# Two feed-forward layers as seven half-size block products each, with activations and block sums kept in DRAM

## The chip, the cores and the metric

The program runs on one core of one Trainium2 chip. The metric is the device time of one execution in microseconds (us). The engines are named as in the profile: PE is TensorE (PEld its weight loads), DVE is VectorE, ACT is ScalarE, POOL is GpSimd and SP is SyncE, which issues most DMAs. SBUF is the on-chip memory with 128 partitions, PSUM the eight accumulators ("banks") of 128 x 512 float32 that PE writes.

## What is computed

Two transformer layers and one state-space block work on 1024 tokens of 1024 features, all in float32. Each of the two layers ends in a gated feed-forward part, and this is what the change touches:

```python
D_FF = 2816
def swiglu(h, w_in, w_out):
    gu = h @ w_in                       # [1024, 1024] @ [1024, 5632]
    gate, up = jnp.split(gu, 2, axis=-1)
    return (jax.nn.silu(gate) * up) @ w_out      # [1024, 2816] @ [2816, 1024]
# in each layer
    h = rmsnorm(x, norm_ffn[i]) * (1 + sc2) + sh2
    x = x + g2 * swiglu(h, ffn_w_in[i], ffn_w_out[i])
```

The first layer's attention (windowed) stands before its feed-forward part, the second layer's (dilated) between the two feed-forward parts, and the state-space block behind the second. That block needs tables made from its parameters alone (discretised matrices, rotations, Toeplitz strips).

## The kernel before

Activations are feature-major: a tile holds 128 features and 512 tokens (half of the tokens, called half 0 and half 1). A float32 product is made as three passes: each operand is split into a rounded part "hi" (a copy on ACT, L448) and the rest "lo" (a subtraction, mostly on DVE, L449), and PE adds hi hi, hi lo and lo hi into one bank. One pass is a matmul of 128 x 128 weights against 128 x 512 activations.

`ffn` (L1054) walks over the 22 tiles of 128 columns of D_FF in ten chunks. For a tile it loads the gate and the up columns, splits them, runs `col_gemm_steps` (L496, matmuls L502 to L504) for both halves of the tokens over eight tiles of features, applies the gate (L1082 to L1087), and at the end of a chunk `row_gemm` (L508, matmuls L488 to L490) multiplies the chunk's activations with its rows of w_out and adds to x in SBUF (L520). So there are 22 x 2 x 2 x 8 x 3 = 2112 matmuls into the hidden width and 22 x 8 x 2 x 3 = 1056 out of it, 3168 in a layer.

At each chunk's end one step of other work is called (`extra`): in the first layer the modulation vectors of the second (`adas`, 48 blocks of 512 KB loaded through tag `wr` and summed on DVE, L268), in the second the tables of the state-space block (`ssm_params`, L1104, written to DRAM: `scalars` on small tiles, `combo` L1303 and L1305, `rots` L1356 to L1362).

The norm ahead of a feed-forward part (`norm`, L385) is a generator that is advanced during `row_gemm` of the attention's output: squares of x, their column sums (PE, L368), 1/rms (small DVE steps, L332 to L339), its spreading over the partitions (PE, L379), then for each of eight feature tiles a scaling (DVE, L428), hi (ACT, L439) and lo (DVE, L442). The later half's last steps stay in `pending` and run during the first matmuls of `ffn`. The norm behind the second layer is `mix_norm` (L1390, L1391, L1406, L1409).

A planner orders each engine's instructions: of those that are ready by its own account, the one that stands first in the program goes first. At run time each engine and each DMA queue works in that fixed order. Tiles of one tag share a fixed number of buffers: 28 slabs of 128 x 1024, two each of `wr`, `wh`, `wl`, `o4` and `tmp`, four each of `s` and `pt`.

## Time and profile before

| | |
|---|---|
| time, median of three runs | 2835.63 us (2835.03 to 2835.66) |
| profiled execution, first to last instruction (span) | 2824.5 us |
| the median beyond that span | 11.1 us |
| PE busy | 2696.7 us, 95% of the span |
| DVE busy | 1648.9 us, 58% |
| ACT busy | 996.4 us, 35% |
| POOL busy | 406.3 us, 14% |
| DMA | 235.97 MB, mean 84 GB/s |

The first feed-forward part lies at about 448 to 1185 us, the second at 1645 to 2375 us. A busy share is an average over all stages; what a stage is worth has to be read from windows inside it.

### The profile page before, as it was taken

What the parts mean: (1) busy time and instruction counts of PE and PEld (TensorE: products, weight loads), DVE (VectorE), ACT (ScalarE), POOL (GpSimd) and SP (SyncE); (2) the same over time, 40 slices, a digit from 0 to 9 for tenths busy, and PEclk for the clock granted to TensorE, in tenths of its full rate; (3) what the DMA queues carried; (4) which work ended last, traced back from release to release, by engine and by line L of the source; (5) the groups of instructions that cost most, each with busy time, mean ns of one, the idle gap of its engine ahead of it and who ended that gap; (6) DMA issues with size and microseconds to landing.
All of it is one profiled execution on the core that took longest, in us unless ns stands there. A gap on an engine that the chain in (4) does not pass through costs nothing.

```text
span 2824.5 us, 32756 instructions
## 1 busy us (share of the span) xinstructions
PE 2696.7 (95%) x12494; PEld 2208.4 (78%) x12494; DVE 1648.9 (58%) x3031; ACT 996.4 (35%) x1820; POOL 406.3 (14%) x518
## 2 busy tenths in 40 slices
PE   4999999999999999988899899999999999999998
PEld 4777778888888888767787678888788887988877
DVE  7788776555564333565666777465554636266355
ACT  4577643111111112377888431111111123224231
POOL 1355521000000000123333200000100003020000
PEclk8999999999999999999999999999999999999999
DMA  7332331333341112211122321121221221261131
GB/s 269 102 97 87 124 101 46 104 117 114 117 129 45 45 45 75 75 38 39 39 61 55 121 61 45 60 69 66 78 69 60 69 75 49 86 209 52 42 144 61
DMA packets 234141, 235.97 MB, mean 84 GB/s; under 512 B 53912, under 2 KB 195968, under 8 KB 233600
## 3 DMA queue, kind: packets, MB, share of 16 engines
q1 hardware_dynamic: 228272, 214.91, 24.6%
q0 software_dynamic: 5312, 18.88, 2.1%
q8 instruction: 98, 1.61, 0.2%
q14 instruction: 59, 0.48, 0.1%
q10 hardware_dynamic: 400, 0.09, 0.0%
HBM read 197.51 MB, written 34.24 MB: 82 GB/s over the span
## 4 chain that ended last, share of the span: by engine, by line
PE 77%; DVE 10%; ACT 5%; DMA 3%; issue 3%; POOL 2%; SPq 0%; ACTq 0%; DVEq 0%; POOLq 0%
PE psg L503 13%; PE psg L502 13%; PE psg L504 13%; PE pssc L489 3%; PE pssc L488 3%; PE pssc L490 3%; PE pstp L488 3%; PE pstp L489 3%; PE pstp L490 3%; PE psg L488 3%; PE psg L490 3%; PE psg L489 3%; PE pso L682 2%; POOL s L136 2%; PE pstp L668 2%
## 5 line engine op out<-in xcount | busy, mean ns | idle before, releaser
L502 PE MATMUL psg<-hh,wh 128*128 128x512 f32 x1888 | 745.6, 396 | 2.8 <-ACT hh L439 2.3
L503 PE MATMUL psg<-hl,wh 128*128 128x512 f32 x1888 | 741.5, 393 | 3.3 <-DVE hl L442 3.2
L504 PE MATMUL psg<-hh,wl 128*128 128x512 f32 x1888 | 740.9, 393 | 1.1 <-DVE wl L449 1.1
L503 PEld LDWEIGHTS psg<-hl,wh 128*128 128x128 f32 x1888 | 357.3, 189 | 76.9 <-DVE hl L442 7.7
L504 PEld LDWEIGHTS psg<-hh,wl 128*128 128x128 f32 x1888 | 356.7, 189 | 76.2 <-DVE wl L449 1.9
L502 PEld LDWEIGHTS psg<-hh,wh 128*128 128x128 f32 x1888 | 356.8, 189 | 73.6 <-ACT hh L439 3.0
L448 ACT CAST wh<-wr 128x1024 fp32r<-128x1024 f32 (+1 forms) x150 | 152.4, 1017 | 608.3 <-PE psg L503 460.3
L449 DVE TENSOR_TENSOR wl<-wr,wh 128x1024 fp32r<-128x1024 f32 (+1 forms) x133 | 159.1, 1196 | 233.6 <-ACT wh L448 233.5
L1084 ACT ACTIVATE tg<-psg 128x512 f32<-128x512 f32 x88 | 52.3, 594 | 545.1 <-PE psg L504 543.6
L1082 DVE TENSOR_TENSOR tg<-tg,psg 128x512 f32<-128x512 f32 x88 | 60.4, 686 | 231.8 <-PE psg L504 231.7
L126 ACT ACTIVATE s<-s,nm 128x256 f32<-128x256 f32 (+4 forms) x320 | 162.5, 511 | 37.7 <-DVE nm L122 32.7
L399 POOL TENSOR_TENSOR nacc<-nacc,nsq 128x512 f32<-128x512 f32 x30 | 40.5, 1350 | 796.7 <-ACT nsq L397 796.6
L520 DVE SCALAR_TENSOR_TENSOR x<-pssc,hf,x 128x512 f32<-128x512 f32 x160 | 119.4, 746 | 58.3 <-PE pssc L490 57.9
L520 DVE SCALAR_TENSOR_TENSOR x<-pstp,hf,x 128x512 f32<-128x512 f32 x160 | 119.4, 746 | 53.1 <-PE pstp L490 52.9
L692 POOL TENSOR_TENSOR o<-o,ob 64x512 f32<-64x512 f32 x80 | 114.6, 1432 | 226.9 <-ACT o L691 220.2
L488 PE MATMUL pssc<-pt,o 128*128 128x512 f32 x352 | 139.4, 398 | 1.0 <-ACT pt L1086 0.7
L488 PE MATMUL pstp<-pt,o 128*128 128x512 f32 x352 | 138.2, 393 | 0.2 <-DVE x L520 0.2
L489 PE MATMUL pssc<-s,o 128*128 128x512 f32 x352 | 138.3, 393 | 0.0
L490 PE MATMUL pstp<-pt,o 128*128 128x512 f32 x352 | 137.6, 391 | 0.0
L490 PE MATMUL pssc<-pt,o 128*128 128x512 f32 x352 | 137.2, 390 | 0.0
L489 PE MATMUL pstp<-s,o 128*128 128x512 f32 x352 | 137.1, 390 | 0.0
L1085 DVE SCALAR_TENSOR_TENSOR tg<-tg,psg 128x512 f32<-128x512 f32 x88 | 60.1, 683 | 113.8 <-ACT tg L1084 113.8
(426 smaller groups left out, 4864.4 us busy)
## 6 DMA issues: line engine op xcount, KB each, us to landing
adaw<-in_ada_w_dram SPq DMA_DIRECT2D x96, 512.0 KB, 3.7
wr<-in_ffn_w_in_dram SPq DMA_DIRECT2D x88, 512.0 KB, 3.8
wr<-in_ffn_w_out_dram SPq DMA_DIRECT2D x44, 512.0 KB, 3.2
wr<-in_w_in_dram SPq DMA_DIRECT2D x24, 512.0 KB, 3.9
xs<-x SPq DMA_DIRECT2D x16, 512.0 KB, 4.0
x<-xs SPq DMA_DIRECT2D x16, 512.0 KB, 4.4
wr<-in_b_w_in_dram SPq DMA_DIRECT2D x12, 512.0 KB, 3.7
xraw<-in_x_dram SPq DMA_DIRECT2D x8, 512.0 KB, 4.7
```

The source lines that it names most:

```text
L126: self.net.nc.scalar.activation(s[:, 0:w], s[:, 0:w], AF.Exp, bias=self.nm[:, i:i + 1], scale=0.125, accum_out=self.l[:, i:i + 1])
L448: self.nc.scalar.copy(hi, raw)
L449: (eng or self.nc.vector).tensor_sub(lo, raw, fl(hi))
L488: nc.tensor.matmul(ps, whi, xhi, start=(a == 0), stop=False)
L489: nc.tensor.matmul(ps, whi, xlo, start=False, stop=False)
L490: nc.tensor.matmul(ps, wlo, xhi, start=False, stop=(a == n - 1))
L502: nc.tensor.matmul(ps, hi[:, k, :], xhi, start=(k == 0), stop=False)
L503: nc.tensor.matmul(ps, hi[:, k, :], xlo, start=False, stop=False)
L504: nc.tensor.matmul(ps, lo[:, k, :], xhi, start=False, stop=(k == KT - 1))
L520: nc.vector.scalar_tensor_tensor(xx, ps, g[:, m:m + 1], xx, op0=ALU.mult, op1=ALU.add)
L692: nc.gpsimd.tensor_add(oap, oap, b)
L1082: nc.vector.tensor_mul(th, th, ps)
```

## The change

Both products of a feed-forward part are made by Winograd's form of Strassen's scheme: the operands are cut into 2 x 2 blocks, and seven block products with sums of blocks replace the eight.

`ffn` becomes two functions. `ffn_wide` makes the hidden activations: tokens are cut in halves, features in halves, and gate against up columns take the place of the two column blocks. It needs seven forms of the normed input (B11, B21, T1 to T4, B22), which `block_norm` makes in place of `norm`: 28 slabs, so x leaves SBUF (to `xd`). For each of 22 column tiles seven products of 12 matmuls run; weight sums are made on POOL, hi and lo parts on ACT and DVE, and partial results are added outside PSUM. The gated activations go to DRAM (`acts`), and POOL also makes block sums of w_out, which go to DRAM as well (`sums`).

`ffn_narrow` multiplies by w_out in seven products of 11 steps with 12 matmuls each. Every step loads half a tile of weights or weight sums, forms block sums of activations on POOL, and splits both operands. x comes back from `xd`.

`adas` now runs in `ffn_wide` of the first layer, one block at every third product, through tag `wl`. `ssm_params` is cut in two parts: one in each `ffn_narrow`, listed by product, traced with a priority 1500 places back (`behind`); its tables pass through DRAM between the two. The norms behind take their tiles of half 1 in the order 4 to 7, 0 to 3, and run within the last product.

The diff, cut to its core (comments that it drops, and changes of names, are left out):

```diff
+    def block_norm(self, x, sb, done):
+        def plain(name, k, src):
+            hi, lo = parts(name, k)
+            nc.scalar.copy(hi, src)
+            nc.vector.tensor_sub(lo, src, fl(hi))
+        def half(hf, order=range(KT)):
...
+            for k in range(4):
+                for i in range(2):
+                    scaled(v[k][i], 4 * i + k, 1, R)
+                nc.vector.tensor_sub(v[k][0], v[k][0], u[k])
+                nc.vector.scalar_tensor_tensor(t2[k], v[k][1], sb(1)[:, 4 + k:5 + k], v[k][0], op0=ALU.add, op1=ALU.subtract)
+                plain("T2", k, t2[k])
+                yield
+            done(1)
+            for k in range(4):
+                plain("T1", k, v[k][0])
+                yield
+            for j in range(KT):
+                nc.vector.scalar_tensor_tensor(u[j], u[j], sb(1)[:, j:j + 1], t2[j % 4], op0=ALU.add, op1=ALU.subtract)
+                yield
+            for j in range(KT):
+                plain("T3" if j < 4 else "T4", j % 4, u[j])
+                yield
+            for k in range(4):
+                shifted("B22", k, 4 + k, v[k][1])
+                yield
-    def ffn(self, i, h, then, extra=()):
+    def ffn_wide(self, i, H, also):
...
+        def operand(at, q, n):
+            g, u = raws[q]
+            if n == 0:
+                sum1[q] = self.slab("tmp", name="sum1")[:, lo_half]
+                nc.gpsimd.tensor_add(sum1[q], u[:, lo_half], u[:, hi_half])
+                nc.gpsimd.tensor_sub(u[:, lo_half], u[:, lo_half], g[:, lo_half])
+            if n == 2:
+                nc.gpsimd.tensor_sub(g[:, lo_half], sum1[q], g[:, lo_half])
+            if n == 6:
+                nc.gpsimd.tensor_sub(g[:, hi_half], g[:, hi_half], g[:, lo_half])
...
+            nc.scalar.copy(t[:, lo_half], src)
+            nc.vector.tensor_sub(t[:, hi_half], src, fl(t[:, lo_half]))
...
+        def take(q, n):
...
+            if n in (0, 2, 4):
+                nc.scalar.copy({0: g0, 2: g1, 4: u0}[n], ps)
+            if n == 1:
+                nc.vector.tensor_add(g0, ps, g0)
+                gate(q, 0)
+            if n == 4:
+                nc.vector.tensor_add(u1, bank[q, "V"], u0)
+            if n == 5:
+                nc.vector.tensor_add(u0, ps, u0)
+                nc.vector.tensor_mul(u0, u0, g0)
+            if n == 6:
+                nc.vector.tensor_add(g1, ps, g1)
+                gate(q, 1)
+                nc.vector.tensor_mul(u1, u1, g1)
+                nc.sync.dma_start(acts[q], ev[q][:, 1, :])
+        def weight_sums(f):
...
+            nc.gpsimd.tensor_add(b[:, hi_half], b[:, hi_half], a[:, hi_half])
+            nc.gpsimd.tensor_sub(a[:, hi_half], a[:, hi_half], a[:, lo_half])
+            nc.gpsimd.tensor_sub(a[:, lo_half], b[:, hi_half], a[:, lo_half])
+            nc.gpsimd.tensor_sub(b[:, lo_half], b[:, lo_half], a[:, lo_half])
...
+        order = [(q, n) for q in range(2) for n in range(2)] + [(q, n) for q in range(2) for n in range(2, 7)]
+        order += [(q, n) for q in range(2, NF) for n in range(7)]
+        AHEAD = 7
...
+            if q > 1 and n == 3 and q % 2 == 0:
+                weight_sums(q // 2 - 1)
+            if q > 1 and at % 3 == 0 and also:
+                also.run(1)
...
+    def ffn_narrow(self, i, acts, sums, xd, then, also):
...
+        PRODUCTS = (
+            ("1", lambda f: w_out[f * P:(f + 1) * P, lo_half], s11, None, [(0, 0)]),
+            ("2", lambda f: w_out[(f + NK) * P:(f + NK + 1) * P, lo_half], s21, None, [(0, 0)]),
+            ("5", lambda f: sums[f, 1][:, hi_half], s11, s12, [(4, 1), (0, 1)]),
+            ("6", lambda f: sums[f, 0][:, lo_half], s11, s22, [(0, 1)]),
+            ("4", lambda f: w_out[(f + NK) * P:(f + NK + 1) * P, hi_half], s21, s11, [(4, 0)]),
+            ("7", lambda f: sums[f, 0][:, hi_half], s12, s22, [(4, 0), (4, 1)]),
+            ("3", lambda f: sums[f, 1][:, lo_half], s22, None, [(0, 1)]),
+        )
...
+            nc.gpsimd.tensor_sub(dst[f], a, b)          # combine(c), for 5, 6, 4, 7
...
+            for into, tag, t, eng in ((wpart, "pt", raw.pop(c), nc.gpsimd if name in "123" else nc.vector),
+                                      (bpart, "s", src[f], nc.vector)):
...
+                nc.scalar.copy(o[:, lo_half], t)
+                eng.tensor_sub(o[:, hi_half], t, fl(o[:, lo_half]))
+        FETCH, COMBINE, SPLIT = 7, 4, 3
...
+            if f % 2 and also.get(name):
+                with self.behind():
+                    also[name].pop(0)()
...
+                        nc.vector.scalar_tensor_tensor(xx, bk[m], gain[:, m0 + m:m0 + m + 1], xx, op0=ALU.mult, op1=ALU.add)
...
+        first = {"1": [load, scalars], "2": [do(couts, 0), do(rots, 0)], "5": [do(couts, 1)], "6": [do(bins, 0)], "4": [do(rots, 1)],
+                 "7": [do(toep, 0), save]}
+        second = {"1": [restore, do(bins, 1), do(toep, 1), do(bins, 2)], "2": [do(couts, 2), do(rots, 2)], "5": [do(couts, 3)],
+                  "6": [do(toep, 2)], "4": [do(rots, 3)], "7": [do(bins, 3), do(toep, 3)]}
```

## Rows read from the trace of the kernel before

**Rows 1.** The page, part 1: engine, busy us (share), instructions; span first.
```profile
span 2824.5 us, 32756 instructions
PE 2696.7 (95%) x12494; PEld 2208.4 (78%) x12494; DVE 1648.9 (58%) x3031; ACT 996.4 (35%) x1820; POOL 406.3 (14%) x518
```

**Rows 2.** Busy time by stretch: stretch and length, busy us (instructions), clock, DMA share, GB/s.
```profile
900.00:1000.00 100.00, 100.00 (x442) 82.50 (x441) 40.88 (x52) 13.50 (x16) 0.00 (x0) 1.00 0.12 37
1000.00:1100.00 100.00, 100.00 (x442) 82.48 (x441) 36.01 (x43) 16.00 (x19) 0.00 (x0) 1.00 0.16 48
```

**Rows 3.** Groups by line: out<-in, shapes, count, then busy us and mean ns.
```profile
L520 DVE SCALAR_TENSOR_TENSOR x<-pssc,hf,x 128x512 f32<-128x512 f32 x160 | 119.4, 746 | 58.3 <-PE pssc L490 57.9
L268 DVE SCALAR_TENSOR_TENSOR tmp<-adaw,cond,tmp 128x1024 f32<-128x1024 f32 x84 | 112.0, 1333 | 21.4 <-DMA adaw<-in_ada_w_dram 20.8
L1082 DVE TENSOR_TENSOR tg<-tg,psg 128x512 f32<-128x512 f32 x88 | 60.4, 686 | 231.8 <-PE psg L504 231.7
L1084 ACT ACTIVATE tg<-psg 128x512 f32<-128x512 f32 x88 | 52.3, 594 | 545.1 <-PE psg L504 543.6 <-DVE s L1087 1.5
L279 DVE TENSOR_REDUCE adar<-psg 128x4 f32<-128x512 f32 x12 | 8.1, 683 | 0.1
```

**Rows 4.** One line's instructions: duration in ns, shortest/median/longest (L399, engines POOL and DVE).
```profile
L399 POOL TENSOR_TENSOR nacc<-nacc,nsq x30: 1261/1294/1745, 409.5 to 1632.7; 128x512 f32<-128x512 f32 x30
L399 DVE TENSOR_TENSOR nacc<-nacc,nsq x12: 675/682/694, 422.1 to 1638.6; 128x512 f32<-128x512 f32 x12
```

**Rows 5.** Timelines of DVE and of POOL: start us, us, instruction; 2372 to 2375.
```profile
2372.76 0.75 DVE L1391 SCALAR_TENSOR_TENSOR nacc<-nsq,f,nacc 128x512 f32<-128x512 f32 x1
2373.46 1.75 DVE L1409 TENSOR_TENSOR xnl<-nu,xnh 128x512 fp32r<-128x512 f32 x1
2372.87 1.78 POOL L1390 TENSOR_TENSOR nacc<-nacc,nsq 128x512 f32<-128x512 f32 x1 [1.86 <-ACT nsq L1386]
```

**Rows 6.** Timelines of DVE and of POOL from 2031 us on.
```profile
2031.41 0.74 DVE L520 SCALAR_TENSOR_TENSOR x<-pssc,hf,x 128x512 f32<-128x512 f32 x1
2031.73 2.41 POOL L1305 TENSOR_TENSOR o<-o 128x1024 f32<-128x1024 f32 x1 [18.36 <-DVE o L1303]
```

**Rows 7.** DVE busy on tile `ws` in a stretch; groups by line of the state-space tables.
```profile
1680.00:1735.00 55.00, 23.59 (x141) 1.00 0.30 68
L1303 DVE TENSOR_TENSOR o<-xc,pw 128x1024 f32<-128x1024 f32 x16 | 19.0, 1221 | 1.6 <-DMA d_bin<-o 1.4
L1362 DVE TENSOR_TENSOR o<-o 128x8 f32<-128x8 f32 (+6 forms) x28 | 8.6, 307 | 0.1
L1305 POOL TENSOR_TENSOR o<-o 128x1024 f32<-128x1024 f32 x12 | 29.1, 2424 | 555.4 <-DVE o L1303 475.2 <-PE psg L504 49.2 <-ACT tg L1084 31.1
```

**Rows 8.** Timeline at the start of the first feed-forward part.
```profile
446.67 0.39 PE L502 MATMUL psg<-hh,wh 128*128 128x512 f32 x1
454.42 1.05 PE L379 MATMUL pso<-ident,rs_y 128*128 128x128 f32 x8
455.51 2.06 DVE L428 SCALAR_TENSOR_TENSOR nu<-x,sc,pso 128x512 f32<-128x512 f32 x3 [0.93 <-PE pso L379]
```

**Rows 9.** Busy time by stretch of 10 us behind each feed-forward part (columns of rows 2).
```profile
1190.00:1200.00 10.00, 7.84 (x32) 4.82 (x31) 7.82 (x12) 7.00 (x9) 0.00 (x0) 1.00 0.00 0
1200.00:1210.00 10.00, 8.11 (x30) 5.15 (x29) 9.39 (x12) 7.66 (x9) 0.00 (x0) 0.83 0.04 10
2380.00:2390.00 10.00, 4.28 (x27) 2.62 (x25) 10.00 (x13) 7.99 (x14) 2.33 (x3) 0.97 0.41 113
2390.00:2400.00 10.00, 8.89 (x41) 8.15 (x42) 6.25 (x15) 5.53 (x9) 3.23 (x5) 0.51 0.60 192
```

**Rows 10.** Busy time of the first 100 us (columns of rows 2); DMA issues, KB, us to landing.
```profile
0.00:100.00 100.00, 61.36 (x274) 51.28 (x275) 71.25 (x117) 43.31 (x70) 13.74 (x31) 0.85 0.62 219
xs<-x SPq DMA_DIRECT2D x16, 512.0 KB, 4.0
x<-xs SPq DMA_DIRECT2D x16, 512.0 KB, 4.4
```

343 lines of the change are left out of this document (251 added, 92 removed).

## The prediction

> **What bounds the kernel now.** I read the page's busy shares first: PE is busy for 95% of the span, DVE for 58%, POOL for 14% [rows 1]. Shares are averages, so busy time by stretch came next: inside a feed-forward part PE is busy in all of 100 us and ends 442 matmuls in it, one per 0.226 us, while DVE works about 40 of the 100 us and POOL not at all [rows 2]. So in these stages PE's count of matmuls sets the time, and a matmul taken away there is worth 0.226 us as long as nothing else becomes late. The other engines have room only on average and without POOL; what happens when POOL works beside DVE is read from two timelines [rows 5, 6].
>
> **What is taken away.** A layer's 3168 matmuls become 22 x 84 = 1848 in the wide half and 7 x 11 x 12 = 924 in the narrow half: 396 fewer, 792 in all. At 0.226 us that is 179 us, the whole gain. The moved steps (modulation vectors, state-space tables) keep their matmuls.
>
> **What a subtraction costs now.** The added work is DVE and POOL instructions of 128 x 512. Alone, DVE takes 0.68 us and POOL 1.29 us [rows 4]; DVE instructions in a row start 0.66 us apart (three in 2.06 us) [rows 8]. They don't run beside each other when DVE reads two tiles of SBUF: at 2372.76 L1391 starts on DVE, POOL's addition starts 0.11 us later and takes 1.78 instead of 1.29 us, and DVE's next, L1409, takes 1.75 instead of 0.68 us [rows 5]. The three last 2.45 us from first start to last end, against 0.75 + 1.29 + 0.68 = 2.72 us in sum: they ran one after the other, and the two hand-overs saved 0.27 us. The x update L520, which reads PSUM and one tile of SBUF, keeps its 0.74 us under a POOL addition [rows 6]. So I count DVE's two-tile instructions and POOL's as one resource ("the pair"): one of each takes 1.70 us, two of DVE and one of POOL 2.36 us.
>
> The Trainium skill, SBUF — State Buffer, section "Who interferes with whom", states the same as a rule: a DVE instruction with two SBUF inputs and a GpSimd instruction that reads SBUF exclude each other for the whole instruction, and it speaks against this change. The rows agree, but for the 0.27 us; by the rule to the letter, steps take 1.97 and 2.65 us, which is the slower rival below.
>
> **The wide half.** A column tile has 84 matmuls, 19.0 us. ACT has 12 instructions of 0.59 us [rows 3], 7.1 us: hidden. DVE has seven splits, two gates and two products that read two tiles of SBUF and four additions from PSUM; POOL has four block sums and, on average, two for w_out. The pair needs 6 x 1.70 + 5 x 0.66 = 13.5 us, the PSUM additions 4 x 0.66 = 2.6 us, half of it under POOL: 14.8 us. In the first layer `adas` adds 48 sums of 1.33 us and 12 reductions of 0.68 us [rows 3], 3.3 us a tile: 18.1 us. Both fit into 19.0, so the hidden products are PE-bound; operands are made seven products ahead. Not ahead is the third partial: behind product n=4 ACT copies (0.59), DVE adds (0.69), and only product n=5 (2.7 us) lies before n=6, which waits for it. If a locked pair (1.97) is queued before that addition, PE waits 3.25 - 2.71 = 0.5 us. I take that for every tile in the first layer and for a third of them in the second: 11 + 4 = 15 us. Bounds: 0, and 59 us if nothing overlaps (first layer 21.2 us a tile, 48 us; second 11 us by the chain alone).
>
> **The entries.** Now the feed-forward part starts while half 1 of the norm is under way: 1/rms is spread 8.8 us after the first matmul (446.67 to 455.5) [rows 8]. The new order has 48 matmuls (10.9 us) that need half 0 alone. Then T2 is wanted, and each of its four tiles costs DVE five instructions: 4 x 5 x 0.66 = 13.2 us, with about six splits and takes between them (4 us) ready at 26.0 us. T2's matmuls of two column tiles are 5.4 us, the last 1.4 behind that moment: PE ends them at 27.4 us after 16.3 us of work, 11.1 us idle. T1 follows at once; T3 needs four lows, eight sums and a split more (9 us, to 35.0), PE is through T1 at 32.8: 2.2 us idle. T4 and B22 then stay ahead. 13 us an entry. TensorE's clock can fall after such a stretch (0.51, that is its 1.2 GHz, in the 10 us behind one with PE 43% busy [rows 9]): 1 us more each. 28 us together; bounds 16 (the planner puts other splits behind the norm) and 50.
>
> **The narrow half** has 77 steps of 12 matmuls, 2.71 us, with operands only three steps ahead. In products 1, 2 and 3 DVE splits one operand and POOL the other: 1.70 us. In 5, 6, 4 and 7 DVE splits both and POOL makes a block sum: 2.36 us. Alone, both fit. But the six products before the last (179.1 us of PE) also carry:
> - 24 x updates, 15.8 us, half of them under POOL: 7.9 us;
> - half of the state-space tables. First layer: the small steps 23.6 us and six of 0.68 us, 4.1 us; four `combo` with 2.44 us on DVE and 2.42 us on POOL each; two `rots` of six lines at 8.6/4 us, 12.9 us each [rows 4, 7]: with 1 us of hand-overs off, 72 us. Second layer: eight `combo` and two `rots`, 63 us.
>
> Splits and sums take 22 x 1.70 + 44 x 2.36 = 141.2 us. Sums: 141.2 + 7.9 + 72 = 221 us, 42 over PE's time; 212 us, 33 over, in the second layer. The low priority doesn't help here: by DVE's own time alone (22 x 0.66 + 44 x 1.32 + 15.8 + 63 = 151 of 179 us) the tables fit, so a plan that leaves the exclusion out puts them there. DVE's queue is fixed, and PE waits behind it. 75 us; bounds 0, and 131 us without any overlap.
>
> **The last product and the norm behind.** Its 11 steps take 29.9 us of PE. The pair has 11 x 1.70 = 18.7 us, x updates 4 us, and the norm: in the first layer about 8 POOL additions, 8 L442, 8 L428 half hidden and 1/rms, 20 us; in the second `mix_norm` has a DVE sum to each square too, 30 us. Over by 13 and 23 us. The kernel before already loses 4 and 7 us there (PE idle in rows 9), so 9 and 16 more, of which I let the next stage's opening matmuls hide half: 12 us; bounds 0 and 51.
>
> **DMA.** Added per layer: w_out is read again in parts, block sums and activations are written and read, x too: about 60 MiB. The narrow half needs 23 MiB in the first 119 us, some 205 GB/s; the start of the program held 219 GB/s with the DMA engines 62% busy [rows 10]. All go through SP's queue, seven steps ahead: hidden. `adas` shares `wl` with the w_out sums; SP can stand behind a held buffer for about 13 us (load 4, four sums 5.2, store 4 us), and what is queued behind it, the next w_in load, is wanted a tile (19 us) later. At each seam the first tiles come back from DRAM as slabs fall free during the last tile's products: 2 us, 4 in all.
>
> **Sum.** 179 - (15 + 28 + 75 + 12 + 4 = 134) = 45 us off the profiled span: 2824.5 - 45 = 2779.5; with the 11.1 us by which the median lies above it, 2790.6, rounded to 2790 us, its own range 2740 to 2845.
>
> **Rivals.**
> - *PE stays the bound.* The tables and sums fall where DVE has room, since splits alone need 2.36 of 2.71 us and `behind` lets them slip. Against it: the planner's account above. Only entries and seams are lost: 2835.6 - 179 + 32 = 2689 us. Chance 0.22.
> - *Slower: VectorE and GpSimd one after the other.* Hand-overs save nothing, x updates find no cover, in the narrow half above all; 1.97 (0.68 + 1.29) and 2.65 us (2 x 0.68 + 1.29) a step. Losses: narrow 70 + 61, last product 51, wide 59, entries and seams 32, together 273: 2835.6 - 179 + 273 = 2930 us. It decides from where those two savings in the narrow half (132 x 0.28 = 37 and 16 us) are gone: then losses are 187 and exceed 179. For it: every hand-over in rows 5 is a block; against it: the 0.27 us and rows 6. Chance 0.18. (This is the Trainium skill's rule to the letter.)
> - *The round trip doesn't overlap, so the scheme doesn't do what it says.* Loads of `acts` wait for the last store: store 4.0, load 4.4 [rows 10], first split 1.3 us, 10 us a seam, 19 us: 2809 us. Against it: only one tile's store is late. Chance 0.08.
>
> **How the numbers follow.** The forecast has 0.52. The range reaches from the first rival to part of the slower one, 2685 to 2890 us, and leaves out about 0.2. A measurement of this kernel can tell about 0.2% (6 us) from no change. Faster by more than that: 0.44 of the forecast's 0.52, 0.22, and 0.06 of the last rival's, 0.72; within it 0.06; slower 0.22.
>
> **What would show it.** Right: some 84 matmuls per 19 us in the wide halves; in the narrow halves PE below 90% with DVE near 100% busy, splits of 128 x 512 lasting up to 2 us, and PE's waits put down to splits; about 13 us of PE idle behind each entry with DVE as releaser. Wrong: PE over 97% busy in the narrow halves (first rival); PE waiting for DMA at the seams (last); DVE full in the first layer's wide half too (slower). A DVE subtraction of two SBUF tiles that keeps 0.68 us beside POOL would make the sum wrong at its root.

## The result, and the profile after

The changed kernel takes 2955.2 us (2950.0 to 2959.9 in four runs), the kernel before 2835.3 beside it: 1.0425 times as long, 95% interval 1.041 to 1.0441. The forecast was 2790 us with a range to 2890: the sign was wrong, and the time lies 65 us outside. The gain itself came, 792 matmuls fewer; what the forecast had at 134 us of losses was far more.

The page of the changed kernel, parts 1 and 5 (as [rows 1] and [rows 3]):

```profile
span 2958.2 us, 33846 instructions
PE 2605.7 (88%) x11702; PEld 2109.5 (71%) x11702; DVE 2023.3 (68%) x3389; ACT 1259.5 (43%) x2416; POOL 1033.8 (35%) x936
...
L1173 DVE TENSOR_TENSOR wpart<-wraw,wpart 128x512 fp32r<-128x512 f32 x264 | 261.8, 994 | 83.7 <-ACT wpart L1172 82.1
```

TensorE falls from 95% to 88% busy, GpSimd rises from 14% to 35%. A split on VectorE, 0.68 us alone [rows 4], takes 0.99 us in the mean.

Busy time by stretch (columns as in [rows 2]): the first two column tiles of the first layer, a stretch late in the second wide half, product 2 of either narrow half, and product 3, the last, of either (a narrow half makes its products in the order 1, 2, 5, 6, 4, 7, 3):

```profile
453.60:490.00 36.40, 29.19 (x101) 21.73 (x102) 34.22 (x56) 15.38 (x28) 8.85 (x6) 0.81 0.12 38
490.00:516.00 26.00, 21.41 (x86) 16.63 (x85) 25.29 (x32) 10.76 (x19) 10.03 (x6) 0.93 0.32 103
2070.00:2170.00 100.00, 100.00 (x443) 82.84 (x442) 68.67 (x80) 36.81 (x63) 26.77 (x18) 1.00 0.24 77
990.00:1068.00 78.00, 36.94 (x143) 28.09 (x141) 51.42 (x181) 13.58 (x24) 43.46 (x34) 0.76 0.50 154
2225.00:2314.00 89.00, 43.68 (x167) 32.60 (x166) 34.89 (x31) 16.20 (x29) 47.09 (x31) 0.71 0.41 143
...
1208.00:1249.00 41.00, 36.12 (x164) 28.95 (x164) 31.53 (x49) 20.93 (x36) 15.97 (x12) 0.96 0.37 112
2456.00:2507.00 51.00, 40.65 (x181) 32.04 (x180) 34.16 (x53) 19.52 (x32) 19.28 (x14) 0.83 0.22 61
```

The third line is the forecast come true: 443 matmuls in 100 us, TensorE never idle. The fourth and fifth show where it failed. Product 2 has 132 matmuls, 29.9 us; it took 78.4 and 88.4 us, and VectorE was far from full in it (51 of 78, 35 of 89 us). TensorE stood idle for 41.1 and 45.3 us of it; the rest of the loss is the lower granted clock (0.76 and 0.71) and the tables' own matmuls.

To place the loss I count the matmuls of L1185 and L1356 by their start times: 84 are a column tile, 132 a product, and each piece is compared with 19.0 or 29.9 us.

| piece | first layer, us over | second layer, us over | forecast for both |
|---|---|---|---|
| column tiles 1 and 2 (36.4 + 26.0; 35.9 + 29.8) | 24 | 28 | 28 |
| column tiles 3 to 22 | 56 | 28 | 15 |
| products 1, 2, 5, 6, 4, 7 | 75 | 87 | 75 |
| product 3 and the norm | 11 | 21 | 12 |

Together 330 us. The kernel before lost 45 in the same parts: its 3168 matmuls of a layer took 733.3 and 744.2 us from first start to last, where 716 are needed (3168 at 0.226). So 285 us are new against a gain of 179; in the stages between, the two profiled executions differ by a further 25. In wide tiles 3 to 22 the loss comes in lumps, tiles of 25 to 28 us between tiles of 19 to 23. From tile 11 of the second layer on, behind the last weight sum, every tile takes 19.0.

What TensorE waits for in the first wide half, VectorE's longest wait there, and SP's own (us in total, times, longest):

```profile
PE pssc L1185 <- DVE ev L1205: 28.3, 10, 6.2
PE psg L1185 <- ACT ev L1200: 9.3, 4, 4.2
...
DVE tmp L267 <- DMA adaw<-in_ada_w_dram: 40.7, 19, 7.6
...
SPq L1155 <- DVE wpart L1173: 99.8, 36, 11.5
SPq L1224 <- POOL wsum L1222: 65.5, 11, 8.3
```

SP's issues around one lump in the second layer (start us, us):

```profile
1818.36 0.33 SPq L1219 DMA_DIRECT2D wsum<-in_ffn_w_out_dram  x1
1826.85 0.33 SPq L1224 DMA_DIRECT2D wsum<-wsum  x1
1827.22 0.43 SPq L1155 DMA_DIRECT2D wraw<-in_ffn_w_in_dram  x1
1828.21 0.52 SPq L1225 DMA_DIRECT2D wsum<-wsum  x1
1828.83 0.44 SPq L1155 DMA_DIRECT2D wraw<-in_ffn_w_in_dram  x1
```

SP stands from 1818.7 to 1826.9 at a store that GpSimd has yet to make. The w_in loads of the tile after next stand behind it. GpSimd, then ScalarE, then TensorE wait in turn; TensorE's wait at the end of this chain, at 1836, is 6.1 us, behind ScalarE's copy L1200. The store's queue is what readers should see here: no engine is full.

In the first layer the chain runs through `adas`. One lump there, on SP, VectorE and TensorE:

```profile
773.90 0.33 SPq L1224 DMA_DIRECT2D wsum<-wsum  x1
776.59 5.41 SPq L255 DMA_DIRECT2D adaw<-in_ada_w_dram  x3
...
780.35 1.29 DVE L267 SCALAR_TENSOR_TENSOR tmp<-adaw,cond,tmp 128x1024 f32<-128x1024 f32 x1 [7.62 <-DMA adaw<-in_ada_w_dram]
781.55 0.68 DVE L1205 TENSOR_TENSOR ev<-pssc,ev 128x512 f32<-128x512 f32 x1
...
782.29 3.89 PE L1185 MATMUL pssc<-H,wpart 128*128 128x512 f32 x10 [5.55 <-DVE ev L1205]
```

SP stands at a sum's store until 773.9 and issues the rows of `adas` behind it; VectorE waits 7.6 us for them, with the addition L1205 behind that sum, and TensorE waits for the addition.

Waits in product 2, of TensorE and VectorE, first layer and then second:

```profile
PE pso L1453 <- DVE o L1400: 20.5, 1, 20.5
...
DVE o L1397 <- DMA o<-in_ssm_log_dt_dram: 13.1, 1, 13.1
DVE o L1435 <- PE pso L1434: 11.0, 1, 11.0
...
PE pso L1599 <- POOL o L1591: 26.9, 2, 18.9
PE pso L1614 <- POOL o L1591: 8.7, 1, 8.7
...
DVE o L1589 <- DMA o<-ssmp: 24.5, 1, 24.5
```

All of these are steps of the state-space tables. TensorE stands in its own queue at a transpose whose data are not there, with the products' matmuls behind it.

### The profile page after: what moved, and what is told of

Read it like the earlier page. It is cut to its first block, busy times and chain, and to the rows that moved or that the text cites. A ratio compares the mean times of both kernels' runs of the same rounds, so it can differ in the third digit from the quotient of the medians.

```text
span 2958.2 us, 33846 instructions
## 1 busy us (share of the span) xinstructions
PE 2605.7 (88%) x11702; PEld 2109.5 (71%) x11702; DVE 2023.3 (68%) x3389; ACT 1259.5 (43%) x2416; POOL 1033.8 (35%) x936
## 5 line engine op out<-in xcount | busy, mean ns | idle before, releaser
L1185 PE MATMUL psg<-H,wpart 128*128 128x512 f32 x1584 | 405.4, 404 | 42.4 <-ACT ev L1200 27.2
L1185 PEld LDWEIGHTS psg<-H,wpart 128*128 128x128 f32 x1584 | 307.5, 196 | 117.8 <-ACT ev L1200 31.4
L1173 DVE TENSOR_TENSOR wpart<-wraw,wpart 128x512 fp32r<-128x512 f32 x264 | 261.8, 994 | 83.7 <-ACT wpart L1172 82.1
L1185 PE MATMUL pssc<-H,wpart 128*128 128x512 f32 x1056 | 268.6, 404 | 35.0 <-DVE ev L1205 34.8
L1185 PEld LDWEIGHTS pssc<-H,wpart 128*128 128x128 f32 x1056 | 205.2, 196 | 84.3 <-DVE ev L1205 40.8
L1185 PE MATMUL pstp<-H,wpart 128*128 128x512 f32 x1056 | 260.6, 395 | 0.0
L1356 PE MATMUL psg<-part,part 128*128 128x512 f32 x792 | 207.0, 409 | 34.8 <-DVE x L1369 14.8
L1185 PEld LDWEIGHTS pstp<-H,wpart 128*128 128x128 f32 x1056 | 201.2, 191 | 42.3 <-DVE nms L434 0.2
L1356 PEld LDWEIGHTS psg<-part,part 128*128 128x128 f32 x792 | 154.7, 198 | 74.2 <-DVE part L1318 18.1
L586 PE MATMUL psg<-hh,wh 128*128 128x512 f32 x480 | 199.9, 417 | 2.2 <-ACT hh L523 1.7
L587 PE MATMUL psg<-hl,wh 128*128 128x512 f32 x480 | 193.2, 402 | 2.1 <-DVE hl L526 2.1
L588 PE MATMUL psg<-hh,wl 128*128 128x512 f32 x480 | 192.4, 401 | 0.0
L1318 DVE TENSOR_TENSOR part<-a,part 128x512 fp32r<-128x512 f32 x154 | 151.3, 990 | 56.0 <-ACT part L1317 54.9
L1200 ACT COPY ev<-psg 128x512 f32<-128x512 f32 x132 | 77.2, 585 | 164.5 <-PE psg L1185 162.8
```

The lines of the kernel that those rows point to most:

```text
L586: nc.tensor.matmul(ps, hi[:, k, :], xhi, start=(k == 0), stop=False)
L587: nc.tensor.matmul(ps, hi[:, k, :], xlo, start=False, stop=False)
L588: nc.tensor.matmul(ps, lo[:, k, :], xhi, start=False, stop=(k == KT - 1))
L1173: nc.vector.tensor_sub(t[:, hi_half], src, fl(t[:, lo_half]))
L1185: nc.tensor.matmul(bank[q, key], a[:, ks], b, start=first and k == m == 0, stop=k == 3 and m == 2, skip_group_check=not first)
L1318: eng.tensor_sub(o[:, hi_half], t, fl(o[:, lo_half]))
```

## The experiments

The theory after the result was **queues**: instructions stand in order behind others that are late (SP's transfers, then GpSimd, ScalarE, TensorE), and buffers and banks with one taker at a time tie them together. The rival was **the pair**, the mechanism of the forecast: VectorE and GpSimd shut each other out and are full. Each run has the kernel before beside it (2829 to 2837 us), and intervals are of the ratio to it. Each run's name stands with its time.

**What the two additions cost.** Weight sums left out, and tables left out:

```diff
-            a, b = [self.slab("wl", name="wsum") for _ in range(2)]
...
-            nc.sync.dma_start(sums[f, 1], b)
```

> Leaves out the weight sums altogether (loads, four GpSimd operations and two stores for each of the 22 pairs); products 5, 6, 7 and 3 of the narrow half take rows of w_out in their place, as many bytes. It bounds what the sums cost. Queue theory: tiles 3 to 22 of the wide halves go to 19 to 20 us each, 70 to 84 us less: 2870 to 2885 us, and not much less than with the stores alone moved. Pair theory: GpSimd's 88 operations of about 1.3 us leave VectorE free for 115 us in all, but in the tiles in which the pair does not bind nothing comes of it; 2900 to 2940 us, and clearly below the run with the stores alone moved.

```diff
-        first = {"1": [load, scalars], "2": [do(couts, 0), do(rots, 0)], ...
+        first = {"1": [lambda: V.memset(self.r8, 0.5), lambda: None], "2": [do(fill, self.d_cout, 0), ...
```

> Leaves out the making of the state-space tables in the narrow halves (their loads, VectorE and GpSimd arithmetic, transposes); each table in DRAM is filled by a copy of rows of w_in_2, issued by GpSimd at the step where the table was made. Queue theory (late loads of the tables' inputs on SP's queue hold VectorE, the tables' transposes hold TensorE's queue and the bank of the fourth accumulator): product 2, 78 and 88 us for its 132 matmuls, falls to 33 to 42 in both narrow halves, and both halves together lose 110 to 150 us: 2805 to 2845 us. Pair theory: what goes is the tables' work on VectorE and GpSimd, 75 us by the forecast: 2880 us, spread over the products that hold the tables and not in product 2 alone.

Measured: 2875.9 us without the sums (e_no_sums; 1.0145, 1.013 to 1.016), 79 less than the changed kernel; tiles 3 to 22 at 19.0 to 21.7 us. In the first wide half VectorE now waits 11.4 us for rows of `adas` instead of 40.7, and TensorE 7.4 us for L1205 instead of 28.3.

Without the tables 2831.6 us (e_no_tables; 0.9992, 0.9979 to 1.0005), 124 less: product 2 at 42.8 and 39.2 us, the narrow halves at 234.6 and 234.8 us where they had 295.4 and 317.6. That is 144 us less in the halves. Time was lost elsewhere, since the copies that fill the tables in this run did not stay at their steps: the planner put all twenty at the program's start. A row of that run's issues in its first 100 us:

```profile
d_cout<-in_w_in_dram POOLq DMA_DIRECT2D x4, 512.0 KB, 14.0
```

The first layer's rows of `adas` land there in 16.6 us instead of 9.9, and the feed-forward part begins at 468.4 us, where the changed kernel and all its other variants have 450 to 455. So the sums and the tables, each left out by itself, are 79 + 144 = 223 us of the 285. 144 instead of the pair's 75, 85 of it in product 2, speaks for the queues; but leaving the tables out also takes their work off VectorE and GpSimd, and the runs on the tables below have to part the two. Without tables the six products before the last still lay 40 us over TensorE's time, where the forecast had splits and sums fitting.

**The pair by itself.**

```diff
-(wpart, "pt", raw.pop(c), nc.gpsimd if name in "123" else nc.vector)
+(wpart, "pt", raw.pop(c), nc.vector)
```

> One edit: in products 1, 2 and 3 of the narrow half the weight is split by VectorE and no longer by GpSimd, as in products 5, 6, 4 and 7 already; nothing is left out. Pair theory: a light step holds the pair 1.32 us in place of 1.70, 66 steps, about 25 us less: 2930 us. Queue theory: the splits wait for transfers and table steps, not for the pair; GpSimd's splits were behind late loads as VectorE's are: 2945 to 2960 us.

Measured (e_dve_splits): 2924.0 us (1.0322, 1.0307 to 1.0338), 31 less. Product 1 falls from 37.1 and 36.2 to 30.5 and 30.1 us, product 2 by 8.6 and 5.9. So the pair is real, of about the size that the forecast's step costs give (25 us), and the queue theory alone missed it. It is a small part of the loss as it stands here, with the stalls in place.

**The sums' stores moved to another queue.**

```diff
-            nc.sync.dma_start(sums[f, 0], a)
-            nc.sync.dma_start(sums[f, 1], b)
+            nc.gpsimd.dma_start(sums[f, 0], a)
+            nc.gpsimd.dma_start(sums[f, 1], b)
```

> One edit: the two stores of the weight sums are issued from GpSimd's queue, which has just made them, and no longer from SP's. Nothing else moves and nothing is left out. Queue theory (SP stands behind these stores until GpSimd has made the four sums, and the next w_in loads stand behind them): the 22 issues that hold SP some 7 us each (load of a sum's rows at 1820.2, its store at 1826.8) stop holding the w_in loads; column tiles that took 25 to 28 us go towards 19 to 21, of the 84 us that tiles 3 to 22 of both wide halves lie above 19 us some 50 to 70 go: 2885 to 2905 us. Pair theory (VectorE and GpSimd shut each other out): the same instructions run on both, so 2955 us, within 6.

Measured (e_sum_stores): 2988.5 us (1.0544, 1.0528 to 1.056), 33 more: the theory in this form fell. SP in this run:

```profile
1897.80 0.38 SPq L1213 DMA_DIRECT2D acts<-ev  x1
1914.70 0.33 SPq L1218 DMA_DIRECT2D wsum<-in_ffn_w_out_dram  x1
1916.05 0.33 SPq L1219 DMA_DIRECT2D wsum<-in_ffn_w_out_dram  x1
1916.43 1.39 SPq L1155 DMA_DIRECT2D wraw<-in_ffn_w_in_dram  x2
```

SP now stands 14.9 us (1899.8 to 1914.7) at the next sum's load, which waits for a `wl` buffer until the store before it has landed. The place moved; the ring of two buffers through load, sum and store is what holds.

**GpSimd's sums without their transfers.**

```diff
+            if f == 0:
+                raws["a"], raws["b"] = [self.slab("wl", name="wsum") for _ in range(2)]
...
+            a, b = raws["a"], raws["b"]
-            nc.sync.dma_start(sums[f, 0], a)
-            nc.sync.dma_start(sums[f, 1], b)
```

> Weight sums left out in the first wide half; in the second GpSimd makes its 44 operations on two buffers that were loaded once, with no other transfer and no store; the narrow halves take rows of w_out in place of the sums. So the second wide half has all of GpSimd's work and none of the queue's. Buffer theory: its tiles 3 to 22 stay at 19.0 to 20 us, as without any sums (443.5 us for the half); engine theory: the tiles with sums are again 25 us and more, 470 us for the half.

Measured (e_sum_ops, one execution): the second wide half took 484.7 us, not 443.5. Both theories missed: with no transfer to wait for, the planner put all 44 sums into one stretch.

```profile
1722.00:1799.00 77.00, 43.26 (x170) 34.67 (x170) 37.87 (x33) 13.49 (x24) 66.44 (x48) 0.77 0.20 62
1799.00:1899.00 100.00, 100.00 (x443) 82.81 (x442) 72.00 (x80) 37.70 (x64) 33.01 (x23) 1.00 0.27 85
```

In the first line GpSimd is busy 66 of 77 us, mostly with sums, and the operands' own block sums stand behind them; tiles 3 and 4 took 31.5 and 45.2 us, all others 19.0. So the planner's order on GpSimd's queue can cost as much as SP's. In the second layer of the changed kernel, too, it runs a sum every 16 us (eleven from 1765 to 1939 us), where the program has one in two tiles; in the first layer a sum comes about every second tile.

**The sums in an order written by hand**, four runs. In all, one half-sum (256 of each 512 columns) stands in each column tile, and SP's and GpSimd's instructions are bound to program order:

```diff
+            e = i.ins.engine
+            if e in last:
+                self.tc.add_manual_dep(i.ins, last[e].name, mybir.DependencyInfo(
...
+            if q > 0 and n == 1:
...
+                weight_sums(q - 1, 0)
+            if q > 0 and n == 5:
+                weight_sums(q - 1, 1)
```

> The weight sums, complete, in halves of their columns: one half-sum per column tile in one buffer of wl where a whole one took both, its loads at product 2 of a tile, its four GpSimd operations (256 columns each) at product 4, its stores in the next tile, and SP's and GpSimd's instructions of the wide half bound to program order, the adas loads apart. All bytes and all sums are as in the changed kernel; nothing is left out. Buffer theory (SP stands at a load or a store of the sums because the two wl buffers pass through load, sum and store one after the other, and the w_in loads stand behind it; moving the stores to GpSimd only moved the place where SP stands, 14.9 us at the next load): SP finds its buffer free, tiles 3 to 22 come to 19 to 21 us in the second wide half and 19 to 22 in the first, 50 to 75 us less than 2955: 2880 to 2905 us. Engine theory (GpSimd's sums and VectorE shut each other out): the same columns are summed, 25 us per half more at most in fixed costs, so 2950 to 2975 us.

Measured (e_sum_order): 3023.3 us (1.0671, 1.0652 to 1.069), slower still. GpSimd's wait in the second wide half:

```profile
POOL wsum L1238 <- DMA wsum<-in_ffn_w_out_dram: 193.5, 19, 11.8
```

SP stood at the tile's activation store until TensorE had ended the tile, and the sums' loads came behind it. The next run writes that store two tiles later:

```diff
+            if n == 0 and q > 1:
+                chain(nc.sync.dma_start(acts[q - 2], ev[q - 2][:, 1, :]))
             product(q, n)
             take(q, n)
```

> The weight sums in halves of their columns and in program order as in the run before it that was slower, with one more edit: the store of a tile's activations is written two tiles later. In that run SP stood at this store until TensorE had finished the tile (issue at 1882.5) and the loads of the sums, behind it, landed 11 us after GpSimd had come to them (wait of 10.3 and 11.7 us in front of its first sum). Queue theory: GpSimd finds its rows landed, the second wide half falls from 494 to 440 to 450 us; in the first the adas loads share the wl buffers and it falls from 533 to 465 to 495: 2900 to 2935 us. Engine theory (GpSimd's sums cost their own time wherever they stand): the second half stays above 470.

Measured (e_sum_order2): 2948.8 us (1.0402); second wide half 466.7, most tiles at 19.8 to 20.6 us, a miss on both sides. The first came to 508.7 us, not 465 to 495. In the second layer the lumps are gone, 1 us a tile stays. Then the sums got a buffer of their own:

```diff
-            a, b = [self.slab("wl", name="wsum") for _ in range(2)]
+            t = ev[q][:, 3, :].rearrange("p (r b c) -> p r b c", r=2, b=2)
```

> The weight sums alone, complete, nothing left out. One half-sum (256 of each 512 columns) per column tile as in the two runs in program order before, but in the fourth row of the tile's own output buffer ev, which the changed kernel leaves empty, so that the sums no longer share wl with the adas loads; loads at product 3 of a tile, GpSimd's four operations behind the operand sum of product 3 of the next, where it has the most time before the next one, stores one tile later. Queue theory: no queue stands, the second wide half comes to 440 to 450 us and the first to 455 to 470 (443.5 and 455.8 without sums): 2885 to 2905 us. Engine theory: GpSimd's 88 sums per half in their halves cost 1 us per tile wherever they stand, as the 20.0 us of most tiles in the run before: 465 and 480, 2925 us.

Measured (e_sum_ev): 2933.8 us (1.0343); second wide half 461.0 us, the first 487, both above what the queue theory had. ScalarE's waits there name the rest:

```profile
ACT ev L1209 <- DMA acts<-ev: 24.8, 18, 2.6
```

The two-tiles-later store lands after ScalarE wants the same buffer. The next run writes it two products earlier (its text counts three):

```diff
-            if n == 0 and q > 1:
-                weight_sums(q - 2, 2)
+            if n == 5 and q > 0:
+                weight_sums(q - 1, 2)
```

> The weight sums alone, complete, nothing left out; as the run with the buffer ev before it, with the stores of a tile (activations and half-sum) three products earlier. In that run ScalarE's first copy of each tile waited up to 2.6 us, 24.8 us in 18 tiles of the second half, for the store of the tile two before to land, and TensorE waited 0.7 us per tile for that copy. Queue theory: with the store earlier the second wide half comes to 443 to 450 us (443.5 without any sums) and the first falls by 10 to 20 from 487: 2895 to 2920 us. Engine theory (GpSimd's sums cost about 0.7 us per tile themselves): both halves stay, 2930 us.

Measured (e_sum_ev2): 2913.1 us (1.0296, 1.028 to 1.0312). The second wide half from its third tile on:

```profile
1763.00:2143.00 380.00, 380.00 (x1678) 314.81 (x1677) 265.11 (x300) 141.17 (x240) 206.03 (x163) 1.00 0.47 149
```

TensorE is busy in all of 380 us, 20 tiles of 19.0, with every sum, load and store in place; the half takes 441.5 us, no more than the 443.5 without sums. GpSimd works 206 of the 380 us. That settles the second wide half: the sums' cost was order and buffers, not engine time. The first layer's half stayed at 494.1, where a fall to some 470 was expected; there `adas` also sends loads (last run below).

**The tables.** Inputs earlier; then three steps on bank `o` moved to a later product; then one number:

```diff
+        also["0"]()
         for c in range(SPLIT):
             split(c)
```

> The loads of the tables' inputs (first narrow half) and the reload of the kept tables (second) are issued behind the first loads of the narrow half, at normal priority, and the transposes of the inputs come later as a step of their own; nothing is left out. Load theory (VectorE and TensorE stand at table steps whose loads were issued late): product 2, 78.4 and 88.4 us, falls to 45 to 60 in both halves, 40 to 70 us less: 2885 to 2915 us. Bank theory (product 2's fourth accumulator has the one buffer o only after the table steps that were planned ahead of it have run): the steps still stand there in the same order; the first half gains its late loads, 10 to 20 us, the second less than 10, product 2 of it stays above 75: 2925 to 2945 us.

```diff
-        second = {"1": [restore, do(bins, 1), do(toep, 1), do(bins, 2)], ...
+        second = {"1": [restore], ... "6": [do(bins, 1), do(toep, 1), do(bins, 2), do(toep, 2)], ...
```

> Three of the table steps that use bank o (two sets of input rows, one Toeplitz set) are planned under the fourth product (6) of the second narrow half and no longer under its first; nothing is left out and no operation changes. Bank theory: product 2 of the second half falls from 88.4 to 35 to 45 us, and the product that takes o next behind them, the fifth (4), rises from 33.7 by 30 to 50 us: the stall moves, 2940 to 2965 us in all. Load theory: product 2 stays above 70, since VectorE waits for the reloaded tables in it as before.

```diff
-    def behind(self, n=1500):
+    def behind(self, n=100):
```

> One number: the table steps of the narrow halves are planned 100 places behind where they stand in the program and no longer 1500. All instructions are the same; their order on the queues is not: the steps that use bank o now stand inside the product they were written into (transposes of the inputs at steps 4 to 6 of product 1, the first half's row set at step 7 of product 6, and so on), not behind the first 36 matmuls of the next product that needs o. Bank theory: product 2 falls from 78 and 88 us to 35 to 55, product 3 from 41 and 51 to 33 to 40, and a part comes back in products 1, 6 and 7, in which TensorE now meets the table steps: 40 to 80 us less, 2875 to 2915 us. Pair theory: VectorE and GpSimd do the same work, 2945 to 2965 us.

Measured: inputs earlier (e_tables_early) 2934.4 us (1.0353, 1.033 to 1.0375), product 2 at 64.4 and 80.4: 21 less, what the bank theory had in each number; late loads are a small part. Steps moved (e_bank_moved) 2953.6 us (1.0424, 1.0406 to 1.0442): product 2 of the second layer falls from 88.4 to 48.3, product 4, the next that takes `o`, rises from 33.7 to 71.3. Those two products:

```profile
2220.00:2268.00 48.00, 32.91 (x133) 25.16 (x131) 19.43 (x19) 12.61 (x23) 38.55 (x27) 0.92 0.64 219
2345.00:2417.00 72.00, 43.83 (x185) 33.20 (x183) 34.30 (x79) 18.56 (x33) 10.04 (x5) 0.74 0.23 70
```

The stall goes with the bank: a product's fourth accumulator gets the one buffer `o` only behind the table steps planned ahead of it, and those, planned 1500 places back, come late. Planned 100 places back (e_behind) they run inside the product they were written into: 2915.0 us (1.028, 1.0258 to 1.0302), 40 less. The second layer's product 2 takes 46.5 us, product 3 32.6 and 37.4; products 1 and 7, which now hold table steps, rise to 43.3 and 45.2 and to 33.5 and 39.1. The first layer's product 2 still took 68.3, but for another reason:

```profile
993.90:1062.00 68.10, 35.87 (x133) 26.94 (x131) 67.52 (x143) 13.68 (x24) 42.69 (x29) 0.81 0.42 137
```

VectorE is busy 67.5 of 68.1 us, where the changed kernel had 51.4 of 78. With the queue mended, the forecast's mechanism appears. One more step spread the bank's users and turned the input rows in the second wide half:

```diff
-                 "7": [do(toep, 0), save]}
+        first = {"0": load, ... "2": [do(bins, 0), nop, do(bins, 1)], ... "6": [do(toep, 0)], ... "7": [do(toep, 1), save]}
...
-        d = net.ffn_wide(1, net.H, None)
+        d = net.ffn_wide(1, net.H, Steps(net.turned()))
```

> The tables alone, nothing left out: inputs loaded at the start of the narrow half, the tables planned 100 places behind their step, at most one step on bank o in each of products 1, 6 and 7 (the four sets of input rows are stored unturned in the first narrow half and turned in the second wide half, in its tiles 11 and later, through a wl buffer), and the working tile used in two halves, so that a step does not wait for the store of the one before. Bank theory: product 2 falls to 33 to 42 in both halves, both halves together lose 70 to 110 of the 124 us that leaving the tables out saves, the second wide half rises by less than 8: 2850 to 2890 us. Pair theory: the tables' 75 us on VectorE and GpSimd stay: 2935 to 2960 us.

Measured (e_tables_spread_b): 2909.5 us (1.0266, 1.0243 to 1.0288), 46 less where 70 to 110 were expected, and not clear of e_behind's 2915.0; product 2 at 67.0 and 57.6, with VectorE busy for 65.5 and 53.8 us of it.

**All together.** Three steps towards one kernel. The first joins the edits of e_sum_order2, e_tables_spread_b and e_dve_splits:

> The edits of the three others together (tables spread, planned 100 places behind, sums in half columns and in order with the late activation store) and products 1 to 3 split by VectorE alone; nothing is left out. If the stalls are the queues' and the bank's, the gains add: 70 to 110 (tables), 20 to 55 (sums), 15 to 30 (VectorE splits): 2770 to 2840 us, at or below the kernel before. Pair theory: only the 31 us of the VectorE splits, 2920 us.

The second takes the sums of e_sum_ev and puts the x updates first, the third leaves them in their place (in both the chain of small operations for the first tables is planned further back, 1200 and 3000 places):

```diff
+                        with self.behind(-2000):
-                        nc.vector.scalar_tensor_tensor(xx, bk[m], ...
+                            nc.vector.scalar_tensor_tensor(xx, bk[m], ...
```

> All edits together, nothing left out: sums in the buffer ev, tables spread and planned 100 places behind (the chain of small VectorE operations of the first tables 1200), products 1 to 3 split by VectorE, and the x updates planned ahead of all other VectorE work. In the run with all edits before it TensorE waited 14.7 and 13.9 us in one piece for the x updates of product 2, which stood on VectorE behind that chain and behind rotation tables. Queue theory: the wide halves come to 465 and 450 us, the narrow ones to 260 each: 2790 to 2835 us, at or below the kernel before. Pair theory (VectorE is full in products 2 and 5 of the narrow halves whatever its order): narrow halves 275 each, 2840 to 2870 us.

> As the run before, but the x updates stand where the program has them and the chain of small operations is planned 3000 places behind. Queue theory: the x updates no longer stand behind the chain either; within 8 us of the run before. If VectorE's order is not what TensorE waits for: also the same; if the priority of the x updates alone matters, 10 to 25 us slower, with a wait of 10 us or more for L1399's successor again.

Measured: 2909.5 (e_all, 1.0248), 2866.2 (e_best, 1.0105, 1.0085 to 1.0126) and 2866.7 us (e_best_b, 1.0113). The first missed the queue theory's range and lies near the pair theory's 2920. In it sums, table rows and `adas` shared `wl` again, its wide halves took 510 and 485 us, and with the sums in their own buffer (e_best) they took 487 and 474; that `wl` is the reason was not tested by itself. The second lies in the pair theory's range (2840 to 2870), its narrow halves at 277 and 268 us where that theory said 275. Where the x updates stand made no difference between the last two: in e_best TensorE still waited 14.6 us in one piece for them. Product 2 of its first layer:

```profile
975.00:1034.00 59.00, 33.46 (x132) 25.64 (x131) 57.56 (x142) 13.17 (x24) 28.63 (x22) 0.84 0.48 166
```

VectorE has no room. So its work was moved, not reordered (`far` is the whole chain of small operations, `sc` a part of it):

```diff
-        first = {... "1": [nop, nop, turn, far], "2": [do(bins, 0), nop, do(bins, 1)], ...
+        first = {... "1": [nop, nop, turn, sc, sc], "2": [sc, sc, sc, sc, sc], "5": [sc, sc, sc, sc, end], ...
```

> All edits together with the earlier stores, and the table work levelled over the narrow halves: in the last combined run VectorE was busy 57.6 of 59 us in product 2 of the first half (50.7 of 53 in the second) and 68.8 of 94 in the last three products. The chain of small operations is cut in ten parts over products 1, 2 and 5, and the table sets move towards products 6, 4, 7 and 3; nothing is left out. If VectorE's fill in products 2 and 5 is what is left (pair theory, in these products only): they fall from 59 and 51 to 45 to 52 and 42 to 46 us, the narrow halves to 260 and 258, the wide ones to 470 and 450: 2800 to 2840 us. If something else holds them (a wait for a queue): product 2 stays above 55 with VectorE idle in it, 2845 us.

Measured (e_final): 2832.8 us, level with the kernel before (1.0009, 0.9998 to 1.002). In the profiled executions the second wide half, with its stores earlier, gives 28 us against e_best, the narrow halves 26, and the first wide half, 493.5 where 470 was expected, takes 7 more. Products 2 and 5 go from 59.0 and 50.8 to 54.9 and 43.4 in the first layer, 5 from 45.3 to 34.3 in the second; product 2 of the second, which kept its rotation tables, stayed (52.9 and 54.2). Where VectorE's work left, the time left with it: in these products its fill is the bound. Last, the `adas` loads:

```diff
+                raws.append(self.ada_load(*todo.pop(0)))
+        more()
+        more()
...
+            self.chain(i)
```

> As the last combined run, with one more edit: in the first wide half the adas rows are loaded two steps ahead of their use and stand on SP's queue where the program has them. In that run the first wide half took 493.5 us (455.8 without the sums, with the same adas work) and VectorE waited 34.4 us in 12 places for adas rows whose loads stood on SP behind the store of the half-sum. Nothing is left out. Queue theory: the half comes to 460 to 475 us, 2795 to 2815 us in all, 0.5 to 1.3% below the kernel before. If VectorE's adas work and the sums together fill the tile: 485 us and more, 2825 us.

Measured (e_final_ada): 2804.7 us (2799.3 to 2811.4; 0.9915, 0.99 to 0.993), 0.8% below the kernel before and 5% below the changed one. The first wide half takes 464.5 instead of 493.5 us. VectorE's waits for rows of `adas` are as long in sum as before (34.6 and 34.4 us), but the longest falls from 7.1 to 4.0 us, and TensorE's waits for the addition behind them from 29.3 to 15.6 us. Page, part 1, and products 2 and 5 of both layers:

```profile
span 2798.3 us, 34107 instructions
PE 2563.3 (92%) x11702; PEld 2078.3 (74%) x11702; DVE 2047.2 (73%) x3455; ACT 1260.5 (45%) x2416; POOL 1017.0 (36%) x958
```

```profile
946.90:1003.10 56.20, 35.07 (x138) 26.79 (x136) 54.97 (x120) 13.69 (x24) 31.60 (x22) 0.86 0.58 197
1003.10:1048.00 44.90, 36.59 (x133) 27.96 (x133) 44.28 (x83) 10.98 (x20) 29.01 (x20) 0.88 0.21 71
2125.40:2179.70 54.30, 33.54 (x134) 25.14 (x132) 54.18 (x79) 12.60 (x23) 35.91 (x20) 0.89 0.63 213
2179.70:2214.00 34.30, 33.25 (x132) 26.45 (x133) 34.03 (x29) 13.03 (x23) 33.36 (x19) 0.92 0.37 121
```

The narrow halves stand at 268.0 and 250.9 us, 59 and 42 over TensorE's 209. The forecast for the same six products and the last one was 87 together; here it is 101. VectorE is full in products 2 and 5, which hold 70 of the 101.

## Why the forecast was wrong

**The gain** was right: 443 matmuls in 100 us in the wide halves, 132 in 29.9 us in product 7 of both layers.

**The step that failed first** is the DMA paragraph: "All go through SP's queue, seven steps ahead: hidden". It even had the mechanism and the size, a held buffer of about 13 us with the next w_in load behind it, and dismissed it because that load "is wanted a tile (19 us) later". Two things were missing. The planner, not the program, sets how often: in the second layer a sum every 16 us. And the load is not the only thing behind it. In the second layer GpSimd waits in order for the sum's rows with the operands' sums behind, and ScalarE with its copies behind those. In the first layer the rows of `adas` come behind the sum's store, VectorE waits for them in order, and the addition L1205 stands behind. TensorE's wait for that addition, which the forecast priced at 0.5 us a tile by a locked pair ahead of it, grew to 6.2 us in this way. Tiles 3 to 22 lost 84 us instead of 15; e_sum_ev2 shows that all of it can go in the second layer, and in the first the last run leaves about 25 of 56.

**The step that failed most** is the price of the tables in "The narrow half". It goes with "The moved steps ... keep their matmuls": their count stayed, their cost did not. In the kernel before, the tables had bank `o` free of the products, and TensorE's waits for them in the second feed-forward part come to one row (1645 to 2375 us):

```profile
PE pso L1328 <- POOL o L1305: 2.6, 1, 2.6
```

Here four of seven products take the same bank. The forecast priced the tables by VectorE's and GpSimd's time (42 + 33 us over) and not by the bank, by their late loads or by TensorE's queue. The six products lost 162 us instead of 75, 107 of them in product 2 alone, and leaving the tables out takes 144 us off the narrow halves. The order alone gives back 39 us of that (e_behind); with VectorE's splits in place of GpSimd's and the tables' work spread and moved it is 94 (e_final_ada), and some 50 us are left. So bank and queue are shown as a cause of the stalls, and VectorE's fill, the forecast's mechanism, stands behind them; how the 144 us divide between the two is not shown further. "The low priority doesn't help here" was right for another reason: 1500 places of it make the bank late.

**The pair** was right as a mechanism. Splits in the narrow halves last up to 2.9 us, and taking GpSimd out of 66 steps gave 31 us where the step costs say 25. But as the place of the loss it was wrong: the forecast wanted VectorE "near 100% busy" in the narrow halves, and the trace has it at 51 of 78 and 35 of 89 us where most time is lost. Only with the queues mended does it become the bound. The Trainium skill, SBUF — State Buffer, section "Who interferes with whom", states the exclusion as a lock. The trace of e_final agrees: 0.21 us alone and 1.25 to 1.30 us beside GpSimd for the same small operation (last section).

**The slower rival** named the sign and nearly the time (2930 us), but it rested on the pair too. Its time was reached by other losses, so it is not borne out.

**The entries**: idle time was right, 36.4 - 29.2 and 26.0 - 21.4 us, 11.8 together where 13 was said. Mis-sized was the clock: 1 us was taken, but behind these waits the granted clock, whose two levels are 1.2 and 2.4 GHz, is 0.81 and 0.93 of full speed in the mean of the two stretches. Of the 50.6 us in which TensorE was busy, 47.9 go to the 168 matmuls of the two tiles, which need 38.0 at 0.226: 9.9 us more, of which the clock can explain at most 36.4 x 0.19 + 26.0 x 0.07 = 8.7. The other 2.7 us are 16 matmuls of the norm, not counted by the forecast.

**The seam and the round trip** were right: the first narrow half's first matmuls wait 4.2 us (4 us were taken for both seams), for a VectorE addition of the last tile and not for a transfer, where the rival had 10.

**Chances**: faster had 0.72. All cases of the forecast took the queues as hidden; no rival had one queue behind another as its mechanism, which is why the range ended 65 us short.

## What to carry to other kernels

Price each new instruction twice: by its engine's time, and by who stands behind it while it waits. A store that waits for an engine, on the queue that also feeds that engine, is a chain, and moving it to another queue moves the chain; a buffer of its own and a written order removed it. A step with low priority that takes a shared bank or buffer holds every later taker, so either give it its own or plan it near its place. When stalls of this kind are gone, look at the occupancy again, since the next bound was hidden under them.

## What the runs showed that was not expected

A small VectorE operation is held for a whole GpSimd operation. Timelines of VectorE and of GpSimd in product 2 of the first layer (e_final):

```profile
1018.84 0.21 DVE L1567 TENSOR_TENSOR o<-o 128x32 f32<-128x32 f32 x1
1019.09 1.25 DVE L1568 TENSOR_TENSOR o<-o 128x32 f32<-128x32 f32 x1
1020.37 1.30 DVE L1563 TENSOR_TENSOR o<-o 128x32 f32<-128x32 f32 x1
1021.60 1.30 DVE L1564 TENSOR_TENSOR o<-o 128x32 f32<-128x32 f32 x1
...
1019.01 1.26 POOL L1328 TENSOR_TENSOR a<-a 128x512 f32<-128x512 f32 x1 [3.27 <-DVE part L1338]
1020.35 3.70 POOL L1328 TENSOR_TENSOR a<-a,a 128x512 f32<-128x512 f32 x3
```

Operations of 32 columns that take 0.21 us alone last 1.25 to 1.30 us, one for each of GpSimd's. The chain of such operations in the first table step is so what fills VectorE there: 86 of them take 33 us of this product's 54.9. In the kernel before, GpSimd worked 14% of the span, and the same chain cost 23.59/141 = 0.17 us a piece [rows 7].

That VectorE and GpSimd exclude each other did not stop the wide half: in the 380 us of e_sum_ev2 they are busy 265.1 and 206.0 us, 471 in sum, blocked time counted, and TensorE waits for neither.
